# Routing search of a fused transformer kernel: 80 candidate sums, two token blocks per stage, VectorE and ScalarE in written order

## The chip, the cores and the metric

The kernel runs on one core of a Trainium2 chip. Its engines each work through a queue of their own, in order: TensorE (PE; PEld is its weight load), VectorE (DVE), ScalarE (ACT), GpSimd (POOL) and SyncE (SP), which issues the DMAs here. The metric is the device time of one execution in microseconds (us).

## The reference, cut to what matters

Two transformer blocks over 256 tokens of width 1024. The first has two layers, a convolution and an attention mixer, each followed by the same expert layer, called `peer` in the kernel. The change lies in the choice of the experts:

```
q = (t @ w_q).reshape(n_tok, 8, 2, 128)
sc = einsum("thpd,hpnd->thpn", q, subkeys)          # 8 heads x 2 halves x 128 keys
sv, si = top_k(sc, 16)                              # 16 best keys of each half
cand = sv[..., 0, :, None] + sv[..., 1, None, :]    # 16 x 16 = 256 sums a head
cidx = si[..., 0, :, None] * 128 + si[..., 1, None, :]
top_v, pos = top_k(cand, 16)                        # 16 best sums
idx = take_along_axis(cidx, pos)
g = softmax(top_v)
h = gelu(xc . u_tab[idx]);  out = (g * h) . v_tab[idx]
```

Both lists of 16 are sorted, so the sum of the i-th and the j-th key has (i+1)(j+1)-1 sums that are at least as large. The 16 best lie among pairs with (i+1)(j+1) at most 16.

## The kernel before, in words

All weights stream from HBM as blocks of 512 KB, called units here. For each unit ScalarE writes a rounded high part `wh` (line 127) and VectorE or GpSimd the rest `wl` (line 128), as `lo_on["pat"]` says ("P" GpSimd, "V" VectorE). `c_unit` then runs 24 matmuls with it (lines 159 to 161) and at its end, in `prepare`, has the unit three places later split. There are three buffers each for `wh` and `wl`, so the `wh` of unit n+3 waits until the matmuls of unit n have read theirs.

An expert layer has 16 units of the query projection (`hp` 0 to 15; numbered 0 to 15 below), then 128 units of table u (16 to 143), of which the first two run in the same loop, then 128 of table v. The tables are dense: all 16384 experts are computed, and the routing weights are multiplied in afterwards. So the search runs beside the units. It is a generator, `side`, of which `advance` takes a piece before each unit, by a budget: every `yield` names a price, and a piece ends when the unit's budget (2.1) is used up. The search finds the 16 best of 128 scores for each of 16 half heads (`topk1`, for two blocks of 128 tokens at a time), then for one block after the other adds up 256 sums a head, finds the 16 best (`top16`), takes a softmax (line 478 is its exponential on ScalarE), and finds the key numbers by comparing with 0 to 15 (line 492), multiplying (495) and adding up (499). TensorE transposes the result (502 to 504). Only then the loop `for j` begins to build routing matrices (`onehots`, line 523 and on); that needs 66 of the 126 units that are left.

Beside this `norm_scales` computes the token scales (squares on ScalarE, line 237; a root; a Newton step on VectorE), `spread` brings them into a row with two small matmuls (lines 328 and 329), and `rescale` rescales the activations for table u (lines 562 to 565).

TensorE and SyncE keep the written order in the whole kernel. The queues of VectorE, ScalarE and GpSimd are filled by a planner that orders instructions by a model of their times.

Of the kernel before, what the change touches and what calls it, by code (L numbers as in the profile page):

```python
# [9 lines left out]
F32 = mybir.dt.float32  # L10
# [30 lines left out]
def kernel(ctx: ExitStack, tc: tile.TileContext, a, out):  # L41
# [358 lines left out]
    def peer(layer):  # L400
# [10 lines left out]
        sib = misc[:, 1024:1280].bitcast(BF).rearrange("p (b s k) -> p b s k", b=2, s=16)  # L411
        tv = misc[:, 1280:1408].rearrange("p (h k) -> p h k", h=8)
        tp = misc[:, 1408:1536].bitcast(U32).rearrange("p (h k) -> p h k", h=8)
        pa = misc[:, 1536:1664].bitcast(U32).rearrange("p (h k) -> p h k", h=8)
        pab = misc[:, 1664:1728].bitcast(BF).rearrange("p (h k) -> p h k", h=8)
        iot16 = misc[:, 1728:1736].bitcast(BF)
        ij = misc[:, 1792:2048].rearrange("p (s h k) -> p s h k", s=2, h=8)
        wf = ar(R0 - 9, 1).rearrange("p (b h k) -> p b h k", b=2, h=8)
        dn = sm[:, 16:24]
# [4 lines left out]
        V.tensor_copy(iot16, iota[:, 0:16, 0])  # L424

        def scores(hp):
            bk = bank[3 + (hp // 2) % 2]
# [27 lines left out]
        def side():  # L455
            for hp in range(16):
                while hp >= st["ready"]:
                    yield 9.0
                topk1(hp)
                yield 2.0  # L460
            renew(F32)
            cand = ar(112, 8).rearrange("p (h c) -> p h c", h=8)
            e1 = ar(120, 4).bitcast(BF).rearrange("p (h k s) -> p h k s", h=8, k=16)
            e2 = ar(124, 4).bitcast(BF).rearrange("p (h k s) -> p h k s", h=8, k=16)
            sm2 = e1.rearrange("p h k s -> p (h k s)")[:, 0:256].bitcast(F32)
            V.tensor_copy(sib, si)
            yield 0.5
            for b in range(2):
                c4 = cand.rearrange("p h (i j) -> p h i j", i=16)
                for g in range(0, 8, 4):  # L470
                    V.tensor_tensor(c4[:, g:g + 4], sv[:, b, 2 * g:2 * g + 7:2, :, None].to_broadcast([128, 4, 16, 16]),
                                    sv[:, b, 2 * g + 1:2 * g + 8:2, None, :].to_broadcast([128, 4, 16, 16]), op=ALU.add)
                    yield 1.1
                for h in range(0, 8, 2):
                    top16([(cand[:, g], tv[:, g], tp[:, g]) for g in (h, h + 1)])
                    yield 3.4
                V.tensor_tensor(wf[:, b], tv, tv[:, :, 0:1].to_broadcast([128, 8, 16]), op=ALU.subtract)
                S.activation(wf[:, b], wf[:, b], AF.Exp)
                V.tensor_reduce(dn, wf[:, b], axis=AX.X, op=ALU.add)
                V.reciprocal(dn, dn)  # L480
                V.tensor_tensor(wf[:, b], wf[:, b], dn[:, :, None].to_broadcast([128, 8, 16]), op=ALU.mult)
                yield 0.8
                for s in range(2):
                    if s == 0:
                        V.tensor_scalar(pa, tp, 4, None, op0=ALU.logical_shift_right)
                    else:
                        V.tensor_scalar(pa, tp, 15, None, op0=ALU.bitwise_and)
                    V.tensor_copy(pab, pa)
                    yield 0.5
                    for g in range(0, 8, 4):  # L490
                        hs = slice(g, g + 4)
                        V.tensor_tensor(e1[:, hs], pab[:, hs, :, None].to_broadcast([128, 4, 16, 16]),
                                        iot16[:, None, None, :].to_broadcast([128, 4, 16, 16]), op=ALU.is_equal)
                        yield 1.2
                        V.tensor_tensor(e2[:, hs], e1[:, hs],
                                        sib[:, b, 2 * g + s:2 * g + s + 7:2, None, :].to_broadcast([128, 4, 16, 16]),
                                        op=ALU.mult)
                        yield 0.7
                        V.tensor_reduce(ij[:, s, hs], e2[:, hs], axis=AX.X, op=ALU.add)
                        yield 1.2  # L500
                bk = bank[3]
                T.transpose(bk[:, 0:128], ij[:, 0].rearrange("p h k -> p (h k)"), ident)
                T.transpose(bk[:, 128:256], ij[:, 1].rearrange("p h k -> p (h k)"), ident)
# [54 lines left out]
            state["j"] = j + 1  # L558

        def rescale(c):  # L560
            t = gt[c % 2]
            V.tensor_tensor(t, xq[0][:, c], xq[1][:, c], op=ALU.add)
            V.tensor_tensor(t, t, rbc, op=ALU.mult)
            S.activation(xh[:, c], t, AF.Copy)
            V.tensor_sub(xl[:, c], t, xh[:, c])

        gen = side()
        run = {"credit": 0.0, "live": True}

        def advance(amount):  # L570
# [8 lines left out]
        st["ready"] = 0  # L579
        for hp in range(18):  # L580
            if hp < 16:
                if hp:
                    evac_q(hp - 1)
                advance(2.1)
                c_unit(bank[hp % 3][:, :256], src=xq)
                if hp == 0:
                    norm_scales()
                if hp == 2:
                    spread(bank[7])
                if 5 <= hp < 13:  # L590
                    rescale(hp - 5)
            else:
                if hp == 16:
                    evac_q(15)
                if hp == 17:
                    h_evac(0)
                advance(2.1)
# [11 lines left out]
        for j in range(2, 128):  # L609
# [2 lines left out]
            h_evac(j - 1)  # L612
            going = not run["live"]
            if not going:
                advance(2.1)
            else:
                lo_on["pat"] = "V"
                if 2 <= c < 66:
# [686 lines left out]
```

## Time and profile before

| what | us |
|---|---|
| median of 3 runs | 2200.87 (2200.45 to 2201.38) |
| the profiled execution | 2199.3 |
| its span in the profile | 2197.2 |
| TensorE busy | 2129.4 |
| VectorE busy | 1666.7 |
| ScalarE busy | 1146.8 |
| GpSimd busy | 409.4 |

The two searches lie at about 107 to 290 us and 1036 to 1220 us of the span. A row of a timeline gives the start, the length, the engine, the line, the operation, output <- inputs with partitions x elements, the count of merged instructions, and in brackets the idle time before it and what ended that. Lengths overlap where an engine starts an instruction before the one ahead has written its last results; the distance of two starts then is the time that an instruction takes from its queue. A busy TensorE is not TensorE at its peak, since the ends of matmuls are modelled.

### The profile page before, as it was taken

The numbers are of one execution on the slowest core, as the hardware profiler recorded it, in microseconds if no ns is written. First come the engines' busy times: TensorE is split into PE (matmuls) and PEld (weight loads), VectorE is DVE, ScalarE is ACT, GpSimd is POOL, SyncE is SP. The second block draws the span as 40 slices with busy tenths as digits, with TensorE's granted clock in tenths as the row PEclk, the third lists the DMA queues.
The fourth block names the chain that finished last, engine by engine and source line by source line (L and its number), as shares of the span: only waits on it lengthen the run. The fifth ranks groups of instructions, "written<-read, shape, count | busy, mean of one in ns | idle before, by whom it ended". The sixth has DMA issues, their size and how long they took to land.

```text
span 2197.2 us, 38270 instructions
## 1 busy us (share of the span) xinstructions
PE 2129.4 (97%) x14590; PEld 1940.3 (88%) x14590; DVE 1666.7 (76%) x3107; ACT 1146.8 (52%) x2102; POOL 409.4 (19%) x176
## 2 busy tenths in 40 slices
PE   9999799999999999999997999999999999889999
PEld 8899799999988888887997999999888888768998
DVE  7799968897566666676999688965666666797997
ACT  5455345555555555566553455545555555655443
POOL 0078640000000000053686300000000001550000
PEclk9999899999999999999998999999999999999999
DMA  7586455555667666633554545556676665424664
GB/s 231 172 239 192 134 175 158 156 154 168 207 192 236 207 195 195 192 116 105 176 172 135 173 154 155 155 172 207 195 220 193 194 195 179 146 92 144 185 188 146
DMA packets 109025, 384.44 MB, mean 175 GB/s; under 512 B 11877, under 2 KB 15333, under 8 KB 108585
## 3 DMA queue, kind: packets, MB, share of 16 engines
q1 hardware_dynamic: 108552, 381.81, 56.7%
q8 instruction: 114, 1.87, 0.4%
q14 instruction: 71, 0.57, 0.1%
q10 hardware_dynamic: 288, 0.19, 0.0%
HBM read 374.61 MB, written 7.34 MB: 174 GB/s over the span
## 4 chain that ended last, share of the span: by engine, by line
PE 88%; DVE 4%; issue 3%; POOL 2%; ACT 1%; DMA 1%; SPq 0%; POOLq 0%; ACTq 0%
PE bank L159 15%; PE bank L161 15%; PE bank L160 15%; PE bank L177 12%; PE bank L178 12%; PE bank L181 12%; PE bank L532 3%; POOL wl L128 2%; DVE arena L859 1%; ACT wh L127 1%; PE bank L429 0%; DVE arena L726 0%; DMA x_d<-x 0%; DVE x L243 0%; DMA x<-in_x_dram 0%
## 5 line engine op out<-in xcount | busy, mean ns | idle before, releaser
L127 ACT ACTIVATE wh<-raw 128x1024 fp32r<-128x1024 f32 x691 | 732.2, 1060 | 461.6 <-PE bank L160 221.7
L128 DVE TENSOR_TENSOR wl<-raw,wh 128x1024 fp32r<-128x1024 f32 x537 | 658.9, 1227 | 255.1 <-ACT wh L127 254.3
L159 PE MATMUL bank<-xh,wh 128*128 128x256 f32 x2792 | 807.9, 289 | 19.2 <-ACT arena L553 11.3
L161 PE MATMUL bank<-xh,wl 128*128 128x256 f32 x2792 | 794.2, 284 | 2.3 <-POOL wl L128 1.4
L160 PE MATMUL bank<-xl,wh 128*128 128x256 f32 x2792 | 793.7, 284 | 0.0
L128 POOL TENSOR_TENSOR wl<-raw,wh 128x1024 fp32r<-128x1024 f32 x154 | 390.7, 2549 | 956.7 <-ACT wh L127 947.0
L159 PEld LDWEIGHTS bank<-xh,wh 128*128 128x128 f32 x2792 | 538.8, 193 | 25.1 <-ACT arena L553 12.1
L161 PEld LDWEIGHTS bank<-xh,wl 128*128 128x128 f32 x2792 | 538.3, 193 | 4.9 <-POOL wl L128 3.2
L160 PEld LDWEIGHTS bank<-xl,wh 128*128 128x128 f32 x2792 | 539.2, 193 | 1.5 <-DVE xl L279 0.8
L177 PE MATMUL bank<-wh,ah 128*128 128x512 f32 x1160 | 453.9, 391 | 3.3 <-ACT arena L736 3.3
L178 PE MATMUL bank<-wl,ah 128*128 128x512 f32 x1160 | 452.7, 390 | 0.0
L181 PE MATMUL bank<-wh,al 128*128 128x512 f32 x1160 | 358.2, 390 | 0.0
L177 PEld LDWEIGHTS bank<-wh,ah 128*128 128x128 f32 x1160 | 218.3, 188 | 50.5 <-ACT arena L736 4.2
L181 PEld LDWEIGHTS bank<-wh,al 128*128 128x128 f32 x1160 | 218.3, 188 | 45.7
L186 ACT ACTIVATE ah<-arena 128x256 fp32r<-128x256 f32 x270 | 112.3, 416 | 278.6 <-PE bank L178 276.8
L178 PEld LDWEIGHTS bank<-wl,ah 128*128 128x128 f32 x1160 | 218.4, 188 | 44.5
L187 DVE TENSOR_TENSOR al<-arena,ah 128x256 fp32r<-128x256 f32 x270 | 114.7, 425 | 121.1 <-PE bank L181 109.1
L523 DVE TENSOR_TENSOR x<-iota,ijT 128x1024 f16<-128x1024 f16 x128 | 90.4, 708 | 53.2 <-PE bank L532 53.2
L310 POOL TENSOR_TENSOR top<-x,arena 128x512 f32<-128x512 f32 x4 | 5.1, 1294 | 631.9 <-DVE x L245 631.9
L546 ACT ACTIVATE arena<-bank 128x284 f32<-128x284 f32 (+42 forms) x128 | 38.9, 304 | 130.6 <-DVE arena L544 130.6
L525 DVE TENSOR_TENSOR x<-x,wT 128x1024 f16<-128x1024 f16 x128 | 96.0, 751 | 0.0
L532 PE MATMUL bank<-x 128*128 128x128 f16 x1024 | 81.2, 220 | 0.0
(295 smaller groups left out, 1969.5 us busy)
## 6 DMA issues: line engine op xcount, KB each, us to landing
raw<-in_u_dram SPq DMA_DIRECT2D x256, 512.0 KB, 3.5
raw<-in_v_dram SPq DMA_DIRECT2D x256, 512.0 KB, 3.7
raw<-in_ff_dram SPq DMA_DIRECT2D x66, 512.0 KB, 3.5
raw<-in_wq_dram SPq DMA_DIRECT2D x32, 512.0 KB, 3.6
raw<-in_conv_in_dram SPq DMA_DIRECT2D x23, 512.0 KB, 3.8
raw<-in_conv_out_dram SPq DMA_DIRECT2D x8, 512.0 KB, 3.5
f_d<-arena SPq DMA_DIRECT2D x8, 512.0 KB, 7.2
raw<-in_aq_dram SPq DMA_DIRECT2D x8, 512.0 KB, 3.5
```

The lines of the kernel that those rows point to most:

```text
L127: S.activation(h, r, AF.Copy)
L128: (P if pat[lo_on["i"] % len(pat)] == "P" else V).tensor_sub(l, r, h)
L159: T.matmul(out_ps, hv[:, k], ah[:, k], start=k == 0, stop=False)
L160: T.matmul(out_ps, hv[:, k], al[:, k], start=False, stop=False)
L161: T.matmul(out_ps, lv[:, k], ah[:, k], start=False, stop=k == 7)
L177: T.matmul(bank[4 + b * 2 + n], sh[:, bs], h[:, ns], start=first, stop=False)
L178: T.matmul(bank[4 + b * 2 + n], sh[:, bs], l[:, ns], start=False, stop=False)
L181: T.matmul(bank[4 + b * 2 + n], sl[:, bs], h[:, ns], start=False, stop=last)
L186: S.activation(h, src, AF.Copy)
L187: V.tensor_sub(l, src, h)
L525: V.tensor_tensor(W, E[:, 1:2].to_broadcast(shape), wT[:, c, :, :, None, :].to_broadcast(shape), op=ALU.mult)
L532: T.matmul(bk[:, t * 128:t * 128 + 128], E[:, 0, t // 2, :, t % 2], W[:, q, t // 2, :, t % 2], start=q == 0, stop=q == 1)
```

## The change

Five things change inside `peer`, and they hold for both layers.

1. 80 sums a head in place of 256: first key with all 16, keys 1 to 7 with the first 8, keys 8 to 15 with the first.
2. Both token blocks go through each stage together, the numbers in 16-bit floats with every element doubled (a last axis of 2). One exponential on ScalarE (line 521) takes the place of two. The transposes stand a `yield 4.0` behind the last step.
3. `rescale` writes the product in one unit and the two parts in the next; `norm_scales` does one block behind unit 0 and one behind unit 1.
4. `wl` moves to VectorE for the units split during `hp` 0 to 12 and, in the loop over `j`, from the end of the second search on. Budgets are 2.4 a unit, 0.5 where `rescale` runs, 1.5 where VectorE makes `wl`.
5. From the loop over `hp` to the end of the search VectorE and ScalarE keep the written order.

```
@@ norm_scales
-    def norm_scales():
-        for b in range(2):
+    def norm_scales(blocks=range(2)):
+        for b in blocks:
@@ side
-                    yield 9.0
+                    yield 1.6
                 topk1(hp)
-                yield 2.0
+                yield 2.4
             renew(F32)
+            V.tensor_tensor(cand[:, :, 0:16], v0[:, :, 0:1].to_broadcast([128, 16, 16]), v1, op=ALU.add)
+            yield 0.5
+            V.tensor_tensor(cand[:, :, 16:72].rearrange("p g (i j) -> p g i j", i=7), ...
+            yield 1.1
+            V.tensor_tensor(cand[:, :, 72:80], v0[:, :, 8:16], v1[:, :, 0:1].to_broadcast([128, 16, 8]), op=ALU.add)
+            yield 0.3
+            for g in range(0, 16, 2):
+                top16([(cand[:, i], tvg[:, i], tpg[:, i]) for i in (g, g + 1)])
+                yield 2.1
+            lo_on["pat"], run["amount"] = "V", 1.5
+            V.tensor_tensor(wf, tv, tv[:, :, :, 0:1].to_broadcast([128, 2, 8, 16]), op=ALU.subtract)
+            yield 0.4
+            V.tensor_copy(si2, si[:, :, :, :, None].to_broadcast([128, 2, 16, 16, 2]))
+            yield 1.1
...
             for b in range(2):
...
                 for s in range(2):
...
                     for g in range(0, 8, 4):
+                        V.tensor_tensor(e1, pij[:, s, b, g:g + 4, :, None, :].to_broadcast(four_h),
+                                        iota[:, None, None, 0:16, :].to_broadcast(four_h), op=ALU.is_equal)
+                        yield 0.7
+                        V.tensor_tensor(e2, e1, si2[:, b, 2 * g + s:2 * g + s + 7:2, None].to_broadcast(four_h),
                                         op=ALU.mult)
                         yield 0.7
+                        V.tensor_reduce(ij[:, b, s, g:g + 4], e2.rearrange("p h k i t -> p h k t i"), axis=AX.X, op=ALU.add)
                         yield 1.2
+                if b == 0:
+                    S.activation(wf, wf, AF.Exp)
+            V.tensor_reduce(dn, wf, axis=AX.X, op=ALU.add)
+            V.reciprocal(dn, dn)
+            V.tensor_tensor(wf, wf, dn[:, :, :, None].to_broadcast([128, 2, 8, 16]), op=ALU.mult)
+            yield 4.0
...
@@ rescale
+            if c < 8:
+                V.tensor_tensor(gt[c % 2], xq[0][:, c], xq[1][:, c], op=ALU.add)
+                V.tensor_tensor(gt[c % 2], gt[c % 2], rbc, op=ALU.mult)
+            if c:
+                t = gt[(c - 1) % 2]
+                S.activation(xh[:, c - 1], t, AF.Copy)
+                V.tensor_sub(xl[:, c - 1], t, xh[:, c - 1])
@@ the loops
+        order.enter_context(tc.manual_schedule(engines={mybir.EngineType.DVE, mybir.EngineType.Activation}))
         for hp in range(18):
             if hp < 16:
                 if hp:
                     evac_q(hp - 1)
-                advance(2.1)
+                lo_on["pat"] = "V" if hp < 13 else "P"
+                advance(1.9 if 5 <= hp < 14 else 0.0)
                 c_unit(bank[hp % 3][:, :256], src=xq)
-                if hp == 0:
-                    norm_scales()
+                if hp < 2:
+                    norm_scales([hp])
                 if hp == 2:
                     spread(bank[7])
-                if 5 <= hp < 13:
+                if 5 <= hp < 14:
                     rescale(hp - 5)
...
             if not going:
+                assert j < R0 - 11
+                advance()
+                if not run["live"]:
+                    order.close()
```

What this moves stands below for three places of the first expert layer.

**ScalarE, softmax of the search.** `wh` is the split of a unit, `arena<-bank` the result of a unit. Before, around the second exponential:

```order
L553 ACTIVATE arena<-bank_92 128x256
L127 ACTIVATE wh<-raw 128x1024
L553 ACTIVATE arena<-bank_93 128x256
L478 ACT_TABLE_LOAD
L478 ACTIVATE arena<-arena 128x128
L127 ACTIVATE wh<-raw 128x1024
L553 ACT_TABLE_LOAD
```

Its input, the subtraction of line 477, stands on VectorE behind these:

```order
L448 MAX arena<-top 128x8 x8
L499 TENSOR_REDUCE arena<-top 128x64 x2
L450 MAX_INDEX arena<-arena,top 128x8 x8
L477 TENSOR_TENSOR arena<-arena 128x128
L485 TENSOR_SCALAR arena<-arena 128x128
```

Now ScalarE has one exponential:

```order
L127 ACTIVATE wh<-raw 128x1024
L581 ACTIVATE arena<-bank_93 128x256
L521 ACT_TABLE_LOAD
L521 ACTIVATE arena<-arena 128x256
L127 ACTIVATE wh<-raw 128x1024
L581 ACT_TABLE_LOAD
```

The exponential stands between two splits in both. Its input (line 486) is now written on VectorE ten units earlier.

**VectorE, from the token scales to the spread.** `gt_84` and `gt_85` are the inputs of the two spread matmuls, which TensorE runs behind unit 2. Before:

```order
L254 TENSOR_SCALAR sm<-sm 128x1
L290 TENSOR_SCALAR sm<-sm 128x1
L328 TENSOR_SCALAR gt_84<-ident,sm 128x128
L299 TENSOR_SCALAR sm<-sm 128x1
L252 RECIPROCAL sm<-sm 128x1
L253 TENSOR_SCALAR sm<-sm 128x1
L254 TENSOR_SCALAR sm<-sm 128x1
L290 TENSOR_SCALAR sm<-sm 128x1
L328 TENSOR_SCALAR gt_85<-ident,sm 128x128
```

Now:

```order
L128 TENSOR_TENSOR wl<-raw,wh 128x1024
L297 TENSOR_SCALAR sm<-sm 128x1
L299 TENSOR_SCALAR sm<-sm 128x1
L252 RECIPROCAL sm<-sm 128x1
L253 TENSOR_SCALAR sm<-sm 128x1
L254 TENSOR_SCALAR sm<-sm 128x1
L290 TENSOR_SCALAR sm<-sm 128x1
L128 TENSOR_TENSOR wl<-raw,wh 128x1024
L328 TENSOR_SCALAR gt_84<-ident,sm 128x128
L328 TENSOR_SCALAR gt_85<-ident,sm 128x128
L330 COPY rbc<-bank_99 128x256
```

The two `wl` are those of units 4 and 5. The one of unit 5 now stands ahead of both spread inputs.

**VectorE, finding the key numbers.** Before, for half a token block:

```order
L492 TENSOR_TENSOR top<-arena 128x1024 x2
L495 TENSOR_TENSOR top<-top,arena 128x1024 x2
L499 TENSOR_REDUCE arena<-top 128x64 x2
```

Now `wl` of successive units stands between:

```order
L511 TENSOR_TENSOR top<-top,iota 128x1024
L128 TENSOR_TENSOR wl<-raw,wh 128x1024
L514 TENSOR_TENSOR top<-top,arena 128x1024
L517 TENSOR_REDUCE arena<-top 128x64
L128 TENSOR_TENSOR wl<-raw,wh 128x1024
```

No `wl` stood in VectorE's queue there before; GpSimd's queue holds 35 fewer of them in each expert layer now.

## Rows read from the trace of the kernel before

**Rows 1.** The page's first part: busy us (share) x instructions.

```profile
PE 2129.4 (97%) x14590; PEld 1940.3 (88%) x14590; DVE 1666.7 (76%) x3107; ACT 1146.8 (52%) x2102; POOL 409.4 (19%) x176
```

**Rows 2.** Busy time by window: PE, PEld, DVE, ACT, POOL, PE clock, DMA.

```profile
220.00:250.00 30.00, 17.41 (x122) 16.48 (x121) 29.97 (x73) 8.86 (x13) 12.98 (x6) 0.77 0.31 100
```

**Rows 3.** Waits of TensorE, 100 to 330 us: total, times, longest.

```profile
PE bank L503 <- DVE arena L499: 6.7, 1, 6.7
PE bank L159 <- ACT arena L553: 5.6, 1, 5.6
PE bank L161 <- POOL wl L128: 3.3, 6, 1.2
```

**Rows 4.** Waits of ScalarE, 100 to 330 us.

```profile
ACT arena L478 <- DVE arena L477: 19.0, 2, 16.2
ACT xh L564 <- DVE gt L563: 14.9, 5, 4.7
```

**Rows 5.** Timeline of ScalarE, splits of units 5, 54, 55; 5, 55 of layer 2.

```profile
116.44 1.06 ACT L127 ACTIVATE wh<-raw 128x1024 fp32r<-128x1024 f32 x1 [1.37 <-issue]
...
286.59 1.06 ACT L127 ACTIVATE wh<-raw 128x1024 fp32r<-128x1024 f32 x1 [1.55 <-issue]
289.47 1.06 ACT L127 ACTIVATE wh<-raw 128x1024 fp32r<-128x1024 f32 x1 [1.55 <-issue]
...
1045.88 1.06 ACT L127 ACTIVATE wh<-raw 128x1024 fp32r<-128x1024 f32 x1 [1.37 <-issue]
...
1218.48 1.06 ACT L127 ACTIVATE wh<-raw 128x1024 fp32r<-128x1024 f32 x1 [1.55 <-issue]
```

**Rows 6.** Groups of ScalarE, 116 to 290 us: count, busy, mean ns, idle.

```profile
L127 ACT ACTIVATE wh<-raw 128x1024 fp32r<-128x1024 f32 x51 | 53.9, 1058 | 59.1 <-issue 39.7 <-PE bank L160 11.1 <-POOL wl L128 8.3
```

**Rows 7.** Timeline of TensorE: the spread, then scores behind two units.

```profile
117.23 0.49 PE L329 MATMUL bank<-gt,ones 128*128 128x128 f32 x2 [0.54 <-DMA x_d<-x]
117.56 0.61 PE L429 MATMUL bank<-arena 128*128 128x128 f32 x4
...
130.84 0.61 PE L429 MATMUL bank<-arena 128*128 128x128 f32 x4
...
134.16 0.61 PE L429 MATMUL bank<-arena 128*128 128x128 f32 x4
```

**Rows 8.** Timeline of ScalarE: two sums of squares, then a split.

```profile
109.18 0.66 ACT L237 ACTIVATE junk<-x 128x512 bf16<-128x512 f32 x1
...
110.63 1.06 ACT L127 ACTIVATE wh<-raw 128x1024 fp32r<-128x1024 f32 x1
```

**Rows 9.** Timeline of TensorE: a wait in the second block, and matmuls after it.

```profile
1960.74 1.16 PE L987 MATMUL bank<-ident,arena 128*128 128x128 f32 x6 [2.81 <-DVE arena L980]
...
1963.71 0.41 PE L161 MATMUL bank<-xh,wl 128*128 128x256 f32 x1
1963.92 0.41 PE L159 MATMUL bank<-xh,wh 128*128 128x256 f32 x1
```

**Rows 10.** Groups of VectorE by shape, 108 to 290 us.

```profile
L495 DVE TENSOR_TENSOR top<-top,arena 128x1024 bf16<-128x1024 bf16 x8 | 18.3, 2319 | 0.0
```

**Rows 11.** The same, 225.4 to 241 us, where GpSimd is idle.

```profile
L499 DVE TENSOR_REDUCE arena<-top 128x64 f32<-128x1024 bf16 x3 | 3.5, 1205 | 0.0
...
L495 DVE TENSOR_TENSOR top<-top,arena 128x1024 bf16<-128x1024 bf16 x2 | 1.3, 680 | 0.0
```

**Rows 12.** The page's groups of instructions, whole span.

```profile
L128 DVE TENSOR_TENSOR wl<-raw,wh 128x1024 fp32r<-128x1024 f32 x537 | 658.9, 1227 | 255.1 <-ACT wh L127 254.3
...
L523 DVE TENSOR_TENSOR x<-iota,ijT 128x1024 f16<-128x1024 f16 x128 | 90.4, 708 | 53.2 <-PE bank L532 53.2
```

**Rows 13.** Timeline of VectorE inside the search for the 16 best.

```profile
145.61 0.85 DVE L442 MAX8 arena<-arena 128x8 f32<-128x128 f32 x4
...
148.58 0.07 DVE L444 MATCH_VALUE_LOAD arena<-arena 128x8 f32 x1
...
148.84 0.07 DVE L444 MATCH_VALUE_LOAD arena<-arena 128x8 f32 x1
```

**Rows 14.** Timeline of GpSimd, nine splits in a row.

```profile
200.93 24.24 POOL L128 TENSOR_TENSOR wl<-raw,wh 128x1024 fp32r<-128x1024 f32 x9 [0.25 <-ACT wh L127]
```

More of the change, by code (lines that the diff above doesn't have):

```diff
@@ L410, in peer @@
         si = misc[:, 512:1024].bitcast(U32).rearrange("p (b s k) -> p b s k", b=2, s=16)
[L411 to L417, printed above, removed]
+        si2 = misc[:, 1024:1536].bitcast(F16).rearrange("p (b s k t) -> p b s k t", b=2, s=16, t=2)
+        tv = misc[:, 0:256].rearrange("p (b h k) -> p b h k", b=2, h=8)
+        tp = misc[:, 256:512].bitcast(U32)
+        pa = misc[:, 1536:1792].bitcast(U32)
+        high, low = [misc[:, 1792 + 128 * i:1920 + 128 * i].bitcast(F16) for i in range(2)]
+        ij = ar(R0 - 11, 2).rearrange("p (b s h k t) -> p b s h k t", b=2, s=2, h=8, t=2)
         wf = ar(R0 - 9, 1).rearrange("p (b h k) -> p b h k", b=2, h=8)
-        dn = sm[:, 16:24]
+        dn = sm[:, 16:32].rearrange("p (b h) -> p b h", b=2)
         nc.sync.dma_start(skT, a["sk"][layer])
@@ L466, in side @@
-            V.tensor_copy(sib, si)
-            yield 0.5
-            for b in range(2):
[L469 to L482, printed above, removed]
-                for s in range(2):
[L484 to L489, printed above, removed]
-                    for g in range(0, 8, 4):
[L491 to L496, printed above, removed]
@@ new lines, in side @@
+            cand = ar(112, 5).rearrange("p (g c) -> p g c", g=16)
+            pij = ar(117, 1).bitcast(F16).rearrange("p (s b h k t) -> p s b h k t", s=2, b=2, h=8, t=2)
+            ta, tb = [ar(118, 1)[:, 128 * i:128 * i + 128].bitcast(F16) for i in range(2)]
+            e1 = ar(120, 4).bitcast(F16)
+            e2 = ar(124, 4).bitcast(F16)
+            sm2 = e1[:, 0:256].bitcast(F32)
+            v0, v1 = [misc[:, 0:512].rearrange("p (g s k) -> p g s k", g=16, s=2)[:, :, s] for s in range(2)]
@@ new lines, in side @@
+            yield 0.3
+            tvg = misc[:, 0:256].rearrange("p (g k) -> p g k", g=16)
+            tpg = tp.rearrange("p (g k) -> p g k", g=16)
+            for g in range(0, 16, 2):
[5 more added lines that the diff above has]
+            V.tensor_copy(si2, si[:, :, :, :, None].to_broadcast([128, 2, 16, 16, 2]))
@@ new lines, in side @@
+            yield 1.1
+            V.tensor_scalar(pa, tp, 3, None, op0=ALU.logical_shift_right)
+            V.tensor_copy(high, pa)
+            V.tensor_scalar(pa, tp, 7, None, op0=ALU.bitwise_and)
+            V.tensor_copy(low, pa)
+            yield 1.1
+            pi, pj = [pij[:, s].rearrange("p b h k t -> p (b h k t)") for s in range(2)]
+            V.tensor_scalar(ta, high, 9.0, None, op0=ALU.is_ge)
+            V.tensor_tensor(ta, ta, low, op=ALU.mult)
+            V.tensor_scalar(tb, high, -1.0, 0.0, op0=ALU.add, op1=ALU.max)
@@ L504, in side @@
+            V.tensor_reduce(dn, wf, axis=AX.X, op=ALU.add)
+            V.reciprocal(dn, dn)
+            V.tensor_tensor(wf, wf, dn[:, :, :, None].to_broadcast([128, 2, 8, 16]), op=ALU.mult)
+            yield 4.0
+            for b in range(2):
+                bk = bank[3 + 4 * b]
+                for s in range(2):
+                    T.transpose(bk[:, 128 * s:128 * s + 128], ij[:, b, s].rearrange("p h k t -> p (h k t)"), ident)
                 T.transpose(bk[:, 256:384], wf[:, b].rearrange("p h k -> p (h k)"), ident)
@@ L560, in rescale, with advance @@
         def rescale(c):
[L561 to L565, printed above, removed]
+            if c < 8:
[5 more added lines that the diff above has]
+                V.tensor_sub(xl[:, c - 1], t, xh[:, c - 1])
         gen = side()
-        run = {"credit": 0.0, "live": True}
-        def advance(amount):
+        run = {"credit": 0.0, "live": True, "amount": 2.4}
+        def advance(less=0.0):
+            amount = run["amount"] - less
             run["credit"] = min(run["credit"] + amount, amount)
@@ L579, in peer @@
         st["ready"] = 0
+        order = ExitStack()
+        order.enter_context(tc.manual_schedule(engines={mybir.EngineType.DVE, mybir.EngineType.Activation}))
         for hp in range(18):
```

23 lines of the change are left out of this document (12 added, 11 removed).

## The prediction

> **What bounds the kernel now.** I read the page's busy shares first, then the windows of the search, then who waits there, then timelines. TensorE is busy for 2129.4 of 2197.2 us [rows 1], so all that can be won is some 68 us in which it waits, and what it loses at a lower clock. A good part lies in the two routing searches: in the 30 us from 220 to 250, TensorE is busy for 17.41 us and its granted clock is 0.77, while VectorE is busy for 29.97 [rows 2]. VectorE's load alone does not hold TensorE up, since in the search it makes only numbers that nobody needs yet. What does is seen in the waits [rows 3, 4]. ScalarE stands 16.2 us at the second exponential of the search, because the planner put that in front of the next split while its input (line 477) was far back in VectorE's queue; TensorE first waits 6.7 us for the transposes' input, then 5.6 us behind ScalarE. Earlier ScalarE waits 14.9 us in five places for `rescale`, and TensorE is held up by late `wl` in six places, 3.3 us in all.
>
> How much the searches lose in all I take from two marks. A split starts when the unit three places ahead has ended, so the splits of units 5 and 55 mark the ends of units 2 and 52. They lie 289.47 - 116.44 = 173.03 us apart in the first expert layer and 1218.48 - 1045.88 = 172.60 in the second [rows 5]; the 51 splits from the first to the last are counted in [rows 6]. Without waits the stretch would be: units 3 to 17 with scores, 15 x 3.32 (134.16 - 130.84 [rows 7]) = 49.8; units 18 to 52, 35 x 2.88 (289.47 - 286.59 [rows 5]) = 100.8; unit 2's scores, 3.32 - 2.88 = 0.44; the spread, about 0.5 (its second matmul starts at 117.23 and the scores at 117.56 [rows 7], so 0.33 for one at most and less for the other); three transposes, at the scores' pace about 0.3. That is 151.8. The loss is 21.2 and 20.8 us, 42.0 together. I name 16.1 of the first 21.2 by the waits (6.7 + 5.6 + 3.3 from [rows 3] and 0.54 at the spread [rows 7]); the rest is the lower clock after them and the restarts.
>
> **The change part by part.** *The exponential.* In written order its input stands ten units ahead of it, so ScalarE has nothing to wait for. The two table loads around it are not new: before there were two such pairs. This takes away the waits of 6.7 and 5.6 us and the slow stretch behind them.
>
> *The transposes.* They stand three units behind the last product that they read, some 3 x 2.88 = 8.6 us. VectorE makes that product right behind the `wl` of its unit, so about 5 us remain. Nothing.
>
> *`rescale` and the splits of units 3 to 15 on VectorE.* With GpSimd at rest, VectorE has per unit a `wl` of 1.227 [rows 12], three operations over 256 elements (bounded by 1.205, the sum over 1024 elements [rows 11], and nothing; by its length in proportion 0.3, plus a start, I take 0.4) and one `topk1` in about five units. One `topk1` is 2 x (2 maxima, 3 searches or replacements): four maxima start 0.19 us apart (0.85 for four of which the last runs out [rows 13]), a search every 148.84 - 148.58 = 0.26 [rows 13], so 2 x (2 x 0.19 + 3 x 0.26) = 2.3 us. A unit costs 1.23 + 1.2 = 2.4 us against 3.32, and with a `topk1` 4.7. A `wl` is ready 0.2 + 1.06 + 1.23 = 2.5 us after the unit three places ahead ends, and is needed two units later, so 2 x 3.32 - 2.5 = 4.1 us of delay are free. The overrun of 1.4 fits. ScalarE no longer waits for `rescale`, whose product is a unit old. The six waits of 3.3 us go.
>
> *The 80 sums and the search to its end.* GpSimd splits units 16 to 36 here, nine of which took 24.24 us, 2.69 each [rows 14], against 2.88; VectorE has no queue position that TensorE waits for until unit 37. From unit 14 to 33 TensorE needs 4 x 3.32 + 16 x 2.88 = 59.4 us. VectorE needs 13 `topk1` x 2.3 = 29.9, at most 16 x 1.16 = 18.6 for the 80-wide searches (taken as if they were 128 wide), and three sums, at most 2.32 each if GpSimd's `wl` stretches them as it does line 495 [rows 10]: 7. So 55.5 at most, and VectorE reaches the next stage early. In the stage behind it, units 34 to 50 (17 x 2.88 = 49.0 us), VectorE makes 17 `wl` (20.9), eight compares and eight products in 16 bits with pairs (0.708 as line 523 has it [rows 12] or 0.68 as line 495 without GpSimd [rows 11]: 16 x 0.7 = 11.2), eight sums of 1.205 (9.6), and 16 short ones. For these the trace has no like rows without GpSimd; by the nearest they lie between 0 and 0.7 each, and I take 0.35, so 5.6. Sum 47.3, with a range from 41.7 to 52.9; 3.3 us of delay are free (2 x 2.88 - 2.5). I cost the whole at nothing; without the cover of VectorE's lead it would be up to 3.9 us a layer.
>
> *The spread: the one place that gets worse.* TensorE runs the spread right behind unit 2. Before, VectorE had its inputs almost in time: the wait was 0.54 us. Now `wl` of unit 5 stands ahead of both inputs in VectorE's queue, and unit 5's split starts only when unit 2 has ended. So the spread must wait for a split and a `wl`: from the end of unit 2, 0.2 to the split's start, 1.06 [rows 5], 1.23 [rows 12], two short scalings of about 0.2: 2.8 us in all. ScalarE's two sums of squares stand right ahead of that split (110.63 - 109.18 = 1.45 us [rows 8]); with the split of unit 4 ahead of them they end 1.06 + 1.45 = 2.5 us after unit 1, plus the root and an evacuation of some 0.3 each. That is 3.1 against the unit's 2.88, so up to 0.2 more. I take 2.8, with 2.3 to 3.5 as bounds. Queued behind on VectorE are the copy of the row and the next `wl`; units 3, 4 and 5 have theirs by then, so no second wait follows.
>
> A pause also costs clock here. After a wait of 2.81 us in the second block the matmuls run 1963.92 - 1963.71 = 0.21 us apart [rows 9], where 24 in 2.88 are 0.12: half the clock of 2.4 GHz. Before, 0.54 at this place cost nothing. I take 1.6 us for the slow stretch, with 0 and 2.5 as bounds: 11 to 25 matmuls at 0.09 more are 1.0 to 2.3.
>
> The Trainium skill's page "TensorE: Matmul & The Clock Gate" speaks against this edit: in its section "HAM oscillation — how this bites in real kernels" it says that waits between bursts of matmuls put the engine back to half clock, and that each such fall is paid anew. The row of 2.81 us agrees. But its section "What's actually happening" says that the point at which the clock changes moves between runs of one kernel; by that the 1.6 us may be missing in some executions, and the sum would be 2164.5.
>
> *Later.* The routing matrices begin two units later than before. TensorE sets the pace in that loop and has the same matmuls, so nothing.
>
> **The sum.** Per layer 2.8 + 1.6 = 4.4 us remain of 21.2 and 20.8. Won: 42.0 - 8.8 = 33.2. From the profiled execution, 2199.3, that is 2166.1. The median of the runs is 1.6 above the profiled execution, so 2167.7; I forecast **2167.5**. With the bounds of the spread (2.3 to 6.0 a layer) the forecast's own range is 2163 to 2171.
>
> **The rivals.** *No clock is lost, or no wait at the spread.* For it: 0.54 us cost nothing. Against: the wait is built from three durations that all have rows. It gives 2200.9 - 42.0 + 5.6 = 2164.5, or 2159 without the wait. 0.22.
>
> *VectorE sets the pace from unit 34 on.* If pairs do not help and compare and product take 1.2 us as the sum does [rows 11], the 16 cost 19.3 in place of 11.2, and with the upper end of the short ones VectorE needs 61 us against 49.0, less the free 3.3: 8.7 us a layer. It gives 2185. Against: line 523 has the same form and 0.708. 0.10.
>
> *Slower than before.* VectorE's long operations may be slow by themselves and not because of GpSimd. Then compare and product take 2.319 each [rows 10], 37.1, and the 16 short ones as much, 37.1, with 20.9 and 9.6: 104.7 against 49.0, less 3.3. That is 52 us a layer, in place of the 16.6 won: 2200.9 + 2 x (52.4 - 16.6) = 2272. It ends slower once VectorE's 17 units exceed 49.0 + 3.3 + 16.6 = 68.9 us. Against: with GpSimd idle the same line 495 takes 0.680 [rows 11]. 0.03.
>
> *The change does not do what it says:* ScalarE or TensorE still stands at the exponential or the transposes, since VectorE comes late in the written order too. Keeping two waits of 6.7 + 5.6 a layer, it gives 2167.5 + 24.6 = 2192. Against: ten units lie between. 0.05.
>
> **How the numbers follow.** The forecast has 0.60; the rivals have 0.22, 0.10, 0.03 and 0.05. The range from 2158 to 2180 holds the forecast, the whole first rival and the milder half of the second: about 0.86. 0.2% (4.4 us) is about what a measurement of this kernel can tell from no change. Faster by more: all but the slower rival and half of the last, 0.94; within: 0.03; slower: 0.03.
>
> **What would show it.** Right: ScalarE's longest wait in the search falls from 16.2 us to under 3; line 503's wait is gone; the split of unit 55 comes about 156 us after that of unit 5, in place of 173, of which 4 lie between unit 2 and unit 3; the wait at the spread is 2.3 to 3.5 us and the matmuls behind it run at half clock for some us; compares and products take about 0.7. Wrong: waits of lines 159 or 161 for a `wl` of VectorE from unit 37 on, a `wl` of GpSimd above 2.88, or VectorE idle in its queue at the transposes.

## The result and the profile after

The changed kernel takes 2165.21 us (median of 4 runs, 2164.79 to 2166.07) against 2201.12 before (4 runs): 35.9 us less. The ratio on record is 0.9842, with a 95% interval of 0.9829 to 0.9854; that of the two medians, 0.9837, lies inside. The forecast was 2167.5 with an own range of 2163 to 2171. The profiled execution takes 2165.04 us, its span 2162.9.

The page's first part, to be set beside [rows 1]: TensorE has the same 14590 matmuls and is busy 98% of a shorter span, and nearly half of GpSimd's work is gone.

```profile
PE 2123.0 (98%) x14590; PEld 1938.0 (90%) x14590; DVE 1598.8 (74%) x3167; ACT 1141.7 (53%) x2096; POOL 223.4 (10%) x106
```

The window of [rows 2], 220 to 250 us (PE, PEld, DVE, ACT, POOL, PE clock, DMA share, GB/s): TensorE is busy throughout at full clock, where it had 17.41 us and 0.77.

```profile
220.00:250.00 30.00, 30.00 (x252) 30.00 (x251) 26.12 (x36) 15.69 (x23) 1.05 (x1) 1.00 0.63 191
```

All waits of TensorE from 100 to 330 us, as in [rows 3] (total, times, longest). The three of before are gone; the one of the spread (line 329) is new at this size.

```profile
PE bank L329 <- DVE gt L328: 2.6, 1, 2.6
PE bank L269 <- DVE x L243: 0.3, 1, 0.3
```

Waits of ScalarE in the same stretch, as in [rows 4]. No exponential and no `rescale` stands among them: in the first row ScalarE waits for TensorE to free a buffer, which is what it should do where TensorE sets the pace; for the second the profile shows no releaser.

```profile
ACT wh L127 <- PE bank L160: 59.4, 34, 6.7
ACT wh L127 <- issue: 42.7, 28, 2.0
```

Waits of VectorE there. Its longest, 8.8 us for a `wh`, is the lead that it has over TensorE where it takes over the splits.

```profile
DVE wl L128 <- ACT wh L127: 33.3, 26, 8.8
```

The distances of the new order: the exponential's input (line 486), the exponential (521), the last product (524) and the transpose that reads it (531). The exponential comes 36 us behind its input, the transpose 5 us behind the product, and neither waits.

```profile
210.71 1.99 DVE L486 TENSOR_TENSOR arena<-arena 128x256 f32<-128x256 f32 x1
248.90 0.42 ACT L521 ACTIVATE arena<-arena 128x256 f32<-128x256 f32 x1
269.50 0.42 DVE L524 TENSOR_TENSOR arena<-arena,sm 128x256 f32<-128x256 f32 x1
275.20 0.27 PE L531 MATMUL bank<-ident,arena 128*128 128x128 f32 x1
```

The marks of [rows 5], splits of units 5 and 55 on ScalarE's timeline in the first and the second expert layer:

```profile
116.42 1.04 ACT L127 ACTIVATE wh<-raw 128x1024 fp32r<-128x1024 f32 x1
...
272.18 1.06 ACT L127 ACTIVATE wh<-raw 128x1024 fp32r<-128x1024 f32 x1 [1.55 <-PE bank L160]
...
1029.16 1.04 ACT L127 ACTIVATE wh<-raw 128x1024 fp32r<-128x1024 f32 x1
...
1183.38 1.06 ACT L127 ACTIVATE wh<-raw 128x1024 fp32r<-128x1024 f32 x1 [1.55 <-PE bank L160]
```

They lie 155.76 and 154.22 us apart, against 173.03 and 172.60: 17.27 + 18.38 = 35.65 us won between the marks. Outside them 0.57 (from the first layer's mark to the second layer) and 0.80 (behind the last mark) are given back, some 0.3 of each by three transposes that now run behind the mark; the rest of it I did not trace. 35.65 - 1.37 = 34.3, the difference of the spans.

What remains is at the spread. TensorE's timeline in the first layer and, from 1031.71 on, in the second (start, length, ..., idle before and its releaser). In the first: a wait of 2.63 us, then matmuls 0.21 us apart, then again 0.12 apart.

```profile
116.06 0.28 PE L161 MATMUL bank<-top,wl 128*128 128x256 f32 x1
118.97 0.86 PE L329 MATMUL bank<-gt,ones 128*128 128x128 f32 x4 [2.63 <-DVE gt L328]
119.62 1.06 PE L429 MATMUL bank<-arena 128*128 128x128 f32 x4
...
121.12 0.41 PE L159 MATMUL bank<-top,wh 128*128 128x256 f32 x1
121.34 0.41 PE L160 MATMUL bank<-top,wh 128*128 128x256 f32 x1
...
122.95 0.28 PE L159 MATMUL bank<-top,wh 128*128 128x256 f32 x1
123.07 0.28 PE L160 MATMUL bank<-top,wh 128*128 128x256 f32 x1
...
1031.71 0.71 PE L329 MATMUL bank<-gt,ones 128*128 128x128 f32 x4 [2.63 <-DVE gt L328]
...
1033.07 0.28 PE L159 MATMUL bank<-top,wh 128*128 128x256 f32 x1
1033.19 0.28 PE L160 MATMUL bank<-top,wh 128*128 128x256 f32 x1
```

The second layer has the same wait and no slow matmuls. The windows say the same by the granted clock (the third number from the end of a row): 0.57 and 0.86 in the first layer, which is half clock (1.2 GHz) in a part of each window, and 1.00 (2.4 GHz) in the second.

```profile
119.00:122.00 3.00, 3.00 (x16) 3.00 (x17) 0.54 (x2) 0.00 (x0) 0.00 (x0) 0.57 1.03 337
122.00:125.00 3.00, 3.00 (x24) 3.00 (x24) 0.00 (x0) 0.54 (x1) 0.00 (x0) 0.86 0.79 210
...
1032.00:1035.00 3.00, 3.00 (x28) 3.00 (x28) 0.42 (x1) 0.00 (x0) 0.00 (x0) 1.00 0.94 329
```

That is 3 x 0.43 + 3 x 0.14 = 1.7 us of clock in the first layer and none in the second. VectorE's timeline shows why TensorE waits: the split of unit 5 stands in front of the two scalings (line 328), though VectorE had what they need at 117.2.

```profile
116.98 0.21 DVE L290 TENSOR_SCALAR sm<-sm 128x1 f32<-128x1 f32 x1
117.50 1.23 DVE L128 TENSOR_TENSOR wl<-raw,wh 128x1024 fp32r<-128x1024 f32 x1 [0.30 <-ACT wh L127]
118.64 0.48 DVE L328 TENSOR_SCALAR gt<-ident,sm 128x128 f32<-128x128 f32 x2
```

VectorE's groups from 220 to 270 us (busy, mean ns), where GpSimd rests: the product (line 514) and the compare (511) take 0.69 us each, as line 495 does in [rows 11] and not as in [rows 10].

```profile
L128 DVE TENSOR_TENSOR wl<-raw,wh 128x1024 fp32r<-128x1024 f32 x17 | 20.8, 1223 | 12.8 <-ACT wh L127 12.8
L517 DVE TENSOR_REDUCE arena<-top 128x64 f32<-128x1024 f16 x8 | 9.7, 1218 | 0.2
L514 DVE TENSOR_TENSOR top<-top,arena 128x1024 f16<-128x1024 f16 x8 | 5.5, 689 | 0.1
L511 DVE TENSOR_TENSOR top<-top,iota 128x1024 f16<-128x1024 f16 x8 | 5.5, 685 | 0.0
```

### The profile page after: what moved, and what is told of

Its sections match the earlier page's. It is cut to its first block, busy times and chain, and to the rows that moved or that the text cites. A ratio compares the mean times of both kernels' runs of the same rounds, so it can differ in the third digit from the quotient of the medians.

```text
span 2162.9 us, 38249 instructions
## 1 busy us (share of the span) xinstructions
PE 2123.0 (98%) x14590; PEld 1938.0 (90%) x14590; DVE 1598.8 (74%) x3167; ACT 1141.7 (53%) x2096; POOL 223.4 (10%) x106
## 4 chain that ended last, share of the span: by engine, by line
PE 92%; DVE 4%; ACT 2%; issue 1%; DMA 1%; POOL 0%; SPq 0%; ACTq 0%; POOLq 0%
PE bank L159 16%; PE bank L160 16%; PE bank L161 16%; PE bank L177 12%; PE bank L178 12%; PE bank L181 12%; PE bank L560 3%; ACT wh L127 1%; PE bank L429 1%; DVE arena L898 1%; DVE arena L765 0%; DVE wl L128 0%; DVE x L243 0%; DMA x<-in_x_dram 0%; PE bank L782 0%
## 5 line engine op out<-in xcount | busy, mean ns | idle before, releaser
L128 DVE TENSOR_TENSOR wl<-raw,wh 128x1024 fp32r<-128x1024 f32 x607 | 744.8, 1227 | 299.8 <-ACT wh L127 298.7
L128 POOL TENSOR_TENSOR wl<-raw,wh 128x1024 fp32r<-128x1024 f32 x84 | 204.7, 2439 | 1048.0 <-ACT wh L127 1042.8
L574 ACT ACTIVATE arena<-bank 128x276 f32<-128x276 f32 (+42 forms) x128 | 37.9, 296 | 131.5 <-DVE arena L572 131.5
L553 DVE TENSOR_TENSOR x<-x,wT 128x1024 f16<-128x1024 f16 x128 | 87.6, 685 | 0.0
```

Of the source, the lines that this page charges most:

```text
L128: (P if pat[lo_on["i"] % len(pat)] == "P" else V).tensor_sub(l, r, h)
```

## The experiments

My theory was the prediction's: the written order, with the new distances between a step and its reader, takes the waits away, and what is left is the wait at the spread. The rivals were that one part alone does it (the order, the two steps of `rescale`, the fewer sums, or GpSimd being at rest), with the others for nothing. Each version is the changed kernel with one part altered, but for the same kernel again, the kernel before in written order, no distance (the exponential and the transposes are moved) and the last one, which joins two others. The versions were timed beside the kernel before, in three rounds in which its median lay between 2200.67 and 2201.18, so medians of different rounds can be set side by side. No version takes away the joint passes over both blocks or the 16-bit form alone; what these two are worth by themselves is not shown. The ratios are those on record; they differ by up to 0.0006 from the ratios of the medians.

| version | median us (lowest to highest) | ratio to before, 95% interval |
|---|---|---|
| changed kernel | 2165.21 (2164.79 to 2166.07) | 0.9842 (0.9829 to 0.9854) |
| the same again | 2164.63 (2163.84 to 2167.0) | 0.9837 (0.9823 to 0.9850) |
| planner's order | 2197.42 (2194.56 to 2199.73) | 0.9983 (0.9974 to 0.9993) |
| before, in written order | 2220.2 (2219.81 to 2221.86) | 1.0086 (1.0069 to 1.0103) |
| no distance | 2179.14 (2178.24 to 2181.48) | 0.9904 (0.9889 to 0.9919) |
| `rescale` in one step | 2176.27 (2172.5 to 2176.8) | 0.9887 (0.9872 to 0.9902) |
| 256 sums | 2166.52 (2164.13 to 2167.27) | 0.9841 (0.9828 to 0.9855) |
| late splits on GpSimd | 2166.52 (2164.76 to 2167.12) | 0.9837 (0.9821 to 0.9853) |
| early splits on GpSimd | 2161.93 (2160.33 to 2162.47) | 0.9820 (0.9803 to 0.9836) |
| spread's inputs first | 2161.09 (2160.65 to 2163.31) | 0.9821 (0.9807 to 0.9834) |
| spread late | 2159.79 (2158.27 to 2160.3) | 0.9809 (0.9796 to 0.9822) |
| spread late, early splits on GpSimd | 2157.68 (2155.01 to 2161.45) | 0.9804 (0.9791 to 0.9818) |

**Without the written order.**

```diff
-        order.enter_context(tc.manual_schedule(engines={mybir.EngineType.DVE, mybir.EngineType.Activation}))
```

> The changed kernel with one part undone: the planner again sets VectorE's and ScalarE's order during the search. Theory 1 (the written order is what removes the waits): the planner again puts the exponential in front of a split before VectorE can have its input, so ScalarE stands there for 5 to 15 us a layer and TensorE behind it; 2180 to 2200 us. Theory 2 (the waits went because VectorE has less to do and no GpSimd beside it; order is incidental): within 4 us of the changed kernel, 2163 to 2169.

It came at 2197.42, near the upper end of the first theory's range: of 35.9 us only 3.6 are left against the kernel before beside it. TensorE's timeline shows the largest loss in the first layer (in the second the same wait is 11.2 us):

```profile
240.19 0.58 PE L161 MATMUL bank<-xh,wl 128*128 128x256 f32 x1 [10.88 <-DVE wl L128]
```

And VectorE's shows the cause: the planner sets all eight compares, products and sums ahead of the splits that TensorE needs, and then makes three of these in a row.

```profile
236.34 0.68 DVE L511 TENSOR_TENSOR top<-top,iota 128x1024 f16<-128x1024 f16 x1
237.06 0.69 DVE L514 TENSOR_TENSOR top<-top,arena 128x1024 f16<-128x1024 f16 x1
237.79 1.22 DVE L517 TENSOR_REDUCE arena<-top 128x64 f32<-128x1024 f16 x1
238.93 3.49 DVE L128 TENSOR_TENSOR wl<-raw,wh 128x1024 fp32r<-128x1024 f32 x3
```

So the main wait changed its place: before, ScalarE stood 16.2 us at the exponential; here TensorE stands at a `wl`. Part of the old wait is back too, and TensorE stands 2.2 us behind ScalarE in each layer:

```profile
ACT arena L521 <- DVE arena L486: 5.1, 1, 5.1
```

The order is needed.

**The kernel before, in written order.**

```diff
+        order = ExitStack()
+        order.enter_context(tc.manual_schedule(engines={mybir.EngineType.DVE, mybir.EngineType.Activation}))
         for hp in range(18):
...
+                if not run["live"]:
+                    order.close()
```

> The kernel before with one part added: VectorE and ScalarE keep the written order from the loop over hp to the end of the search. Theory 1 (order alone carries most of the gain): ScalarE's wait of 16.2 us at the exponential is gone and the time is 2168 to 2182 us. Theory 2 (VectorE's relief carries it): VectorE was busy without a break from 130 to 285 us, some 18 us more than 52 units need, so in written order TensorE waits for it at the transposes and ScalarE at rescale and the exponentials; 2190 to 2215.

2220.2, 19 us slower than before and above both ranges. The waits of TensorE and ScalarE from 100 to 330 us, to be set beside [rows 3, 4]:

```profile
PE bank L503 <- DVE arena L499: 18.8, 2, 9.4
PE bank L429 <- ACT arena L437: 5.3, 5, 2.1
...
ACT xh L564 <- DVE gt L563: 20.6, 6, 4.2
```

The transposes hold TensorE 9.4 us in each of the two blocks, since they stand right behind the products. On VectorE the sum of the exponentials waits 7.9 us, as ScalarE comes to the exponential only behind its splits:

```profile
DVE sm L479 <- ACT arena L478: 15.4, 2, 7.9
```

The order alone does harm: in it the transposes, the sum and `rescale` wait, since each stands too close to what it reads.

**No distance between a step and its reader.** The exponential stands right in front of its sum, the transposes a unit behind the last product.

```diff
-                if b == 0:
-                    S.activation(wf, wf, AF.Exp)
+            S.activation(wf, wf, AF.Exp)
             V.tensor_reduce(dn, wf, axis=AX.X, op=ALU.add)
...
-            yield 4.0
+            yield 0.4
```

> The exponential is written right in front of the sum that reads it, and the transposes a unit after the last product, in place of some ten and three units. Theory 1 (a written order needs the distances): VectorE stands at the sum for ScalarE's exponential, which stands behind splits, for 4 to 8 us as in the kernel before in written order (7.9 us), and TensorE then waits for the transposes' input, 3 to 9 us a layer and some half clock: 2171 to 2190. Theory 2 (the order alone is enough, my prediction's view of the transposes at nothing): 2163 to 2167.

2179.14, as the first theory has it, by 13.9 us. TensorE's timeline at the transposes:

```profile
269.60 0.47 PE L529 MATMUL bank<-ident,arena 128*128 128x128 f32 x1 [4.01 <-DVE arena L522]
269.73 0.56 PE L159 MATMUL bank<-xh,wh 128*128 128x256 f32 x1
...
270.51 0.41 PE L159 MATMUL bank<-xh,wh 128*128 128x256 f32 x1
270.73 0.41 PE L160 MATMUL bank<-xl,wh 128*128 128x256 f32 x1
```

The wait is 4.0 us in each layer, and half clock follows: the granted clock is 0.97 from 250 to 270 and 0.91 from 270 to 300 us, 0.6 + 2.7 = 3.3 us. Twice 7.3 is 14.6, against 13.9 measured. I had expected VectorE to wait 4 to 8 us for the exponential; it waited 0.67 us, and the rest is the transposes standing too close. So this version shows what the transposes' distance is worth, and little of the exponential's.

**`rescale` in one step.**

```diff
-            if c < 8:
-                V.tensor_tensor(gt[c % 2], xq[0][:, c], xq[1][:, c], op=ALU.add)
-                V.tensor_tensor(gt[c % 2], gt[c % 2], rbc, op=ALU.mult)
-            if c:
-                t = gt[(c - 1) % 2]
-                S.activation(xh[:, c - 1], t, AF.Copy)
-                V.tensor_sub(xl[:, c - 1], t, xh[:, c - 1])
+            t = gt[c % 2]
+            V.tensor_tensor(t, xq[0][:, c], xq[1][:, c], op=ALU.add)
+            V.tensor_tensor(t, t, rbc, op=ALU.mult)
+            S.activation(xh[:, c], t, AF.Copy)
+            V.tensor_sub(xl[:, c], t, xh[:, c])
...
-                if 5 <= hp < 14:
+                if 5 <= hp < 13:
```

> The changed kernel with rescale in one unit again: sum, product, high and low part together, so that ScalarE stands in its queue until VectorE has the product. If two steps are needed in the written order: ScalarE waits 0.5 to 1.5 us in each of eight units, splits come late and TensorE waits; 2168 to 2176. If not (my view: the product is ready about 3.2 us after the unit's end, the high part at 3.6, the next split at 3.5, and 4 us are free): 2164 to 2167.

2176.27: my view fell, and the other range ends 0.3 below. ScalarE's waits and TensorE's from 100 to 330 us:

```profile
ACT xh L593 <- DVE gt L592: 18.4, 8, 3.5
...
PE bank L429 <- ACT arena L437: 3.2, 2, 2.3
```

ScalarE stands eight times for the product, 2.1 to 3.5 us each, because VectorE makes it behind a split; the evacuation of the queries (line 437) queues behind ScalarE, and TensorE waits for that at the scores (line 429). From 130 to 190 us TensorE is busy for 56.4 of 60 us. Twice 3.6 is 7.2, and the two profiled executions differ by 7.5 (2172.5 against 2165.04). The median is 3.8 above that execution, at a mean clock of 0.991 to 0.992 in place of 0.995; that part no profile shows.

**256 sums.** Four sums of 1024 in place of the three, searches 256 wide, and positions split at 16.

```diff
-            cand = ar(112, 5).rearrange("p (g c) -> p g c", g=16)
+            cand = ar(112, 16).rearrange("p (g c) -> p g c", g=16)
...
```

> The changed kernel with all 256 sums a head again (searches 256 wide, priced 3.4 a pair, sums priced 1.1 each of four), the rest as it is. VectorE needs about 15 us more, the search ends about five units later. If fewer sums are off the critical path (my view): 2164 to 2167, the same as with 80. If VectorE's relief by the 80 sums is what wins: 2172 to 2190.

2166.52: no difference that can be measured, as the intervals lie over each other. VectorE is 32 us longer busy (1630.4 us against 1598.8), and TensorE's waits from 100 to 330 us are the same two as in the changed kernel.

**Late splits on GpSimd** (units 37 and later, until the search ends).

```diff
-            lo_on["pat"], run["amount"] = "V", 1.5
+            run["amount"] = 1.5
```

> The changed kernel, with wl of units 37 and on left on GpSimd to the end of the search, so that it runs beside the compares, products and sums; order and budgets as they are. If GpSimd is what stretches these operations: compare and product take 1.5 to 2.4 us in place of 0.69, the small ones about 2, VectorE needs 70 to 80 us for the 17 units of 49 though it makes no wl, ScalarE waits at the exponential and TensorE at the transposes; 2180 to 2215 us. If the form of the operations decides: VectorE has 20 us less to do, durations stay at 0.69, and the time is that of the changed kernel, 2163 to 2167.

2166.52: the expectation failed, though what it rests on happened. VectorE's groups from 220 to 270 us in this version, beside GpSimd at work:

```profile
L514 DVE TENSOR_TENSOR top<-top,arena 128x1024 f16<-128x1024 f16 x8 | 22.7, 2833 | 0.3
L511 DVE TENSOR_TENSOR top<-top,iota 128x1024 f16<-128x1024 f16 x8 | 12.5, 1568 | 0.0
L517 DVE TENSOR_REDUCE arena<-top 128x64 f32<-128x1024 f16 x7 | 8.5, 1220 | 0.2
```

The products take four times as long. But the 17 splits (20.8 us) are off VectorE, its lead of 8.8 us is there to be used up, and TensorE is busy for 30.00 of 30 us from 220 to 250. The last product of the weights is written at 274.5 us and the transpose that reads it runs at 276.5, 2 us later in place of 5, without a wait. That VectorE makes the late splits brings nothing by itself.

**Early splits on GpSimd** (units 3 to 15).

```diff
-                lo_on["pat"] = "V" if hp < 13 else "P"
+                lo_on["pat"] = "P"
```

> The changed kernel, with wl of units 3 to 15 left on GpSimd, beside rescale. If GpSimd stretches rescale's operations: up to 2.4 us each in place of 0.42, about 5 us a unit with 3.32 to do it in, for eight units; ScalarE's split does not wait since the product is a unit old, but VectorE falls up to 10 us behind and ScalarE then waits for it; at the spread TensorE waits about 0.5 to 1.5 in place of 2.63, since no wl stands ahead of its inputs. 2163 to 2175 us. If two-step rescaling alone was enough: no waits in units 8 to 14 and 2158 to 2163 from the spread.

2161.93, faster than the changed kernel by 3.3 us. `rescale`'s sum and product grow beside GpSimd, from 0.42 to 1.30 and from 0.43 to 0.69 us on average, but ScalarE waits for none of them. With no split ahead of the scalings on VectorE, TensorE's wait at the spread shrinks, and no half clock follows in either layer:

```profile
117.92 0.71 PE L329 MATMUL bank<-gt,ones 128*128 128x128 f32 x4 [1.07 <-DVE gt L328]
```

**The spread.** Its scalings are written behind the second block's scales, ahead of that unit's split, and its matmuls behind unit 2 (inputs first) or unit 3 (late).

```diff
-                if hp == 2:
-                    spread(bank[7])
+                if hp == 1:
+                    for b in range(2):
+                        V.tensor_scalar(gt[b][:, :128], ident, col(b, 5), None, op0=ALU.mult)
+                if hp == 3:      # 2 in the version with the inputs first
+                    for b in range(2):
+                        T.matmul(bank[7][:, b * 128:b * 128 + 128], ones, gt[b][:, :128], start=True, stop=True)
+                    V.tensor_copy(rbc, bank[7][:, :256])
```

> As the last, but with the matmuls still behind unit 2. The scales of the second block end about 1.0 us after unit 2, so a wait of 1.2 to 1.4 us stays. If a wait of this length costs no clock: 2159 to 2161.5, that is 2.6 us above the kernel without the wait. If it costs clock in one layer: about 1.5 more.

> The changed kernel, with the spread's two scalings on VectorE right behind the scales (ahead of the split of unit 5) and its two matmuls behind unit 3 in place of unit 2. If the wait of 2.63 us at the spread and the slow matmuls after it are the price of the written order there: the wait is gone, no slow stretch follows, and 6 to 9 us go, 2156.5 to 2159.5. If the pause is paid elsewhere (the next splits then come late): 2162 to 2166.

2161.09 and 2159.79. The first lies within what was expected if a short wait costs no clock, the second is 0.3 above the 2156.5 to 2159.5 expected without a wait, and far below the other theory's range. With the inputs first the wait is 1.1 us, at full clock; late, there is none. In the late version the marks give the stretch without waits directly (ScalarE's timeline, the first layer, 51 splits):

```profile
118.18 1.05 ACT L127 ACTIVATE wh<-raw 128x1024 fp32r<-128x1024 f32 x1
...
269.51 1.06 ACT L127 ACTIVATE wh<-raw 128x1024 fp32r<-128x1024 f32 x1 [1.55 <-PE bank L160]
```

151.3 us. The prediction had worked out 151.8, of which 0.3 were transposes that now lie behind the mark.

**Both.** The late spread and the early splits on GpSimd together.

> Two of the changes that were faster together: the spread's scalings and products in separate units, and the splits of units 3 to 15 left to GpSimd. Theory 1 (both take away the same wait at the spread): no more than the first alone, 2157.5 to 2160.5. Theory 2 (the second brings something of its own, by a shorter queue on VectorE): 2154 to 2157.

2157.68, but from 2155.0 to 2161.5, with an interval that overlaps that of the late spread alone. Whether the second edit adds something is not settled. Both beat the two kernels.

**The changed kernel once more.**

> The changed kernel once more, unaltered. After the wait of 2.63 us at the spread the first profile showed half clock in the first expert layer and full clock in the second, and the other variants with that wait show both too. Theory 1 (the fall is drawn anew in each execution): another profile may show another pattern, the runs' granted clock moves between 0.992 and 0.994, and their times spread over some 3 us, 2163.5 to 2167. Theory 2 (it belongs to the layer and its code): the same pattern again, times within 1.3 us as before (2164.8 to 2166.1).

Its profile shows the same pattern, half clock in the first layer and none in the second, as theory 2 has it; its times spread over 3.2 us, as theory 1 has it. The granted clock of its five runs speaks for theory 1: the two with a mean of 0.993 took 2166.46 and 2167.00 us, the three with 0.994 took 2163.84 to 2164.63. So executions of one kernel differ in granted clock, and these by 2 to 3 us; one slow stretch costs 1.7. That the stretch at the spread makes the difference is not shown, since only one of the five was profiled, and the four runs in the first row of the table do not part in this way (2164.79 at 0.993, 2165.38 at 0.994).

## Why the prediction was right, point by point

*What bounds the kernel.* Right. The loss of 42.0 us in the searches was read against a stretch without waits; for the first layer the late spread then measured 151.3 us, where 151.5 had been worked out.

*The exponential and the transposes.* Right: the waits for lines 499 and 553 are gone. For the transposes the reason is shown: their wait comes back (4.0 us a layer) where the distance is taken away, and the 5 us that the prediction left them are the 5 us measured. The price of nothing holds only with the three units between. For the exponential the order is shown as the reason by the planner's version, where ScalarE stands 5.1 us at it; how near it may stand to its input was not tried.

*`rescale` and the early splits.* Right that ScalarE no longer waits because the product is a unit old: no `rescale` stands among its waits, and the version in one step pays 7.5 us from profile to profile. My expectation for that version contradicted the prediction's own sentence and was wrong. Not seen was that moving the early splits to VectorE is no gain: left on GpSimd they cost nothing and shorten the wait at the spread.

*The search to its end.* Right at nothing. Compares and products took 0.69 us (0.7 forecast). The third sum, beside GpSimd, took 2.49 where 2.32 was called the most. The rival in which VectorE sets the pace from unit 34 on, and the slower one, did not come. The version with the late splits on GpSimd shows that long products alone do not decide it, as long as the splits are not in the same queue.

*The spread.* The place and the wait were right: 2.63 us in both layers, 2.8 forecast. The failed step is "I take 1.6 us for the slow stretch" in each layer: it was 1.7 in the first and 0 in the second. Against 151.5 us without waits (151.8 less the transposes' 0.3), 155.76 - 151.5 = 4.3 and 154.22 - 151.5 = 2.7 us remain, where 4.4 was forecast twice. The result lies between the forecast and the rival in which no clock is lost (2164.5), and nearer to the rival: 0.7 from it, 2.3 from the forecast. Whether the clock falls behind this wait the prediction could not know, and on which side of the two the median came out is luck.

*The sum.* From profile to profile 34.3 us were won, 33.2 forecast. That is 1.1 of the miss of 2.3. The other 1.2 come from the 1.4 us that I put on top because the median of before lay 1.6 above its profiled execution; the changed kernel's median lies 0.2 above its own.

*The signals.* ScalarE's longest wait did not fall under 3 us: it is 6.7, at the spread, where ScalarE waits for TensorE, which itself stands. I had counted only waits for VectorE. The half clock behind the spread came in the first layer alone. The others came as written: 156 us between the marks (155.8, 154.2), no wait for a `wl` from unit 37 on, GpSimd's splits at 2.44 us on average.

## What to carry to other kernels

In this kernel a written order pays only with distances: a step that another engine reads must stand so far ahead that it is done when the reader's queue comes to the reader, and either part alone was worth little or did harm (the order alone +19 us, the new code in the planner's order -3.6, both -35.9). Less work on an engine that has slack is worth nothing here: 32 us of VectorE's time changed the total by less than the runs spread. After such a change look for the one wait that is left and for what stands ahead of its input; here moving two short scalings and two matmuls brought another 5.4 us.

## What the runs showed of the hardware

The same wait costs clock or not. After a wait of TensorE of 2.6 to 2.8 us at the spread, the time lost to half clock (window by window, one less the granted clock, times the length) was:

| kernel | first layer | second layer |
|---|---|---|
| changed | 1.7 | 0 |
| the same again | 1.7 | 0 |
| late splits on GpSimd | 3.4 | 1.7 |
| 256 sums | 0 | 0 |
| `rescale` in one step | 1.7 | 0 |
| no distance | 0 | 1.7 |

It fell in 6 of 12. After 1.1 us (spread's inputs first, early splits on GpSimd) it fell in none of 4, and after 2.3 us at the scores (`rescale` in one step) in neither layer. After 4.0 us (no distance) it fell in both layers. What draws the line between the 6 and the 6 stays open. The Trainium skill's page "TensorE: Matmul & The Clock Gate", section "What's actually happening", says that the point at which the clock changes varies. Between kernels with the same wait the table agrees; the two profiles of the one kernel show the same pattern.

In the version with late splits on GpSimd the products grow from 0.689 to 2.833 us and the compares from 0.685 to 1.568, while the sums over one input stay at 1.22 (1.218 before that edit). The Trainium skill's page "SBUF — State Buffer", section "Who interferes with whom", says that a VectorE instruction with two inputs in SBUF contends with a GpSimd instruction that reads SBUF, and that a reduction does not; these rows agree.
